# State space phases for half the groups per half of the partitions, on VectorE, and table work dosed behind the weight splits

## The chip, the cores and the metric

One NeuronCore of a Trainium2 chip runs the whole program. The metric is device time in microseconds (us), the median of several runs. TensorE multiplies matrices, VectorE and ScalarE do elementwise work, GpSimd does elementwise work and issues some transfers, SyncE (SP) issues the weight loads.

## What is computed

A stack of three blocks on 256 tokens of 1024 features, in float32: a gated delta rule mixer with a dense SwiGLU feed-forward, a state space (S5) mixer with a mixture of eight experts, and a block of pooling and windowed attention with a wide feed-forward. The change is about the tables of the state space mixer:

```python
dt = exp(log_dt)[:, None]                     # 64 groups, 64 states each
a_bar = exp(lam * dt)                         # complex
b_bar = ((a_bar - 1) / lam)[..., None] * b
h_t = a_bar * h_(t-1) + b_bar u_t             # u: 64 groups of 16 channels
y_t = Re(c h_t) + d * u_t
```

The kernel splits the 256 steps into 64 chunks of four and carries the state from chunk to chunk in a frame that turns with it. For that it needs the phases: the cosine and sine of 4 m Im(lam dt) for m = 0 to 63, for every group and state.

## The kernel before, in words

Weights come from memory in float32 and are used in two parts, a high one (float32r) and the rest. `schedule` lists chunks of 1 MB, two pieces of 128 x 1024 each. `load` (line 296) issues a chunk on SP's queue as soon as one of three buffers is free; `prep` (279) has ScalarE make a piece's high part (290) and VectorE, or GpSimd for the pieces that `pool_splits` names, the low part (292). There are five buffers for parts, and `wget` (314) runs three pieces ahead of the products. `mm3` makes three products of each block (lines 336 to 338).

Side work is written as generators. `spawn` queues one, `tick` (242) runs once for each block of products, and a generator yields how many ticks to let pass. A scheduler at compile time then orders each engine's instructions by the order of the program and by when it expects their inputs; `issue_after` adds an edge that puts an instruction behind another of the same engine. A tile takes the room of an earlier one with the same tag, and waits until nobody uses that one any more.

The dense feed-forward (`ffn`, 967) has 22 blocks of hidden units in groups of 6, 6, 6 and 4. `up(g)` makes a group's hidden units, two pieces and two ticks a block (the first four pieces, two blocks, go tile by tile in `both`, eight ticks, and end in `first`, line 981). `whole(g)` multiplies a group by the second weights, one piece and two ticks a block. The order is up(0), up(1), whole(0), up(2), whole(1), up(3), the loads of the next layer norm's gain and offset (`ln_rows`, 811), whole(2), and the last group, `final`, one token tile after the other. `ln_part` (line 848) adds the residual, `ln_sums` and `ln_apply` (868, 870) normalise, `to_features` (830) turns the rows, and the state space layer `s5` (1235) begins. `ln_rows` loads two rows to one partition on GpSimd's queue (815) and broadcasts them on GpSimd (817). Its tile `gb` shares a tag with `bxy`, and the rows `rr` have the tag `lnr`.

`s5_tables` (1097) runs beside the feed-forward. Four loads are issued at once; six ticks later VectorE begins: two exponentials (`expf`, 1036), a sine and cosine of 448 columns (`sincos`, 1055), powers of the transition, the factor (a - 1) / lam, the input vectors `bxy`, and last the input maps B (1229 to 1232), of which a tick gets one or two operations. The work comes in bunches, with `yield 2` between them. From line 1196 on GpSimd copies six phases (m = 1, 2, 4, 8, 16, 32) into CC and SS and doubles them by products (1209 to 1215), in four generators of 16 groups. Here the partitions hold 64 states twice, once for the real and once for the imaginary part; CC and SS are 128 x 64 groups x 64 chunks, the same in both halves but for a sign in SS.

The pieces that GpSimd splits are 0, 1, 2, 4, 6, 8, 10, 12 of the feed-forward (line 960) and 0, 1, 2 of the state space layer (1032).

Of the kernel before, what the change touches and what calls it, by code (L numbers as in the profile page):

```python
# [42 lines left out]
S5L = dict(per=4, s0=3, m=1, o=0, mb=2, a=2, b=2, c=2, d=4, e=2, f=1, g=1, ct=4, gt=4, keep=2)  # L43
MO = dict(d=3, t=2, b=5, a=2, sc=1)
WARM = dict(a=12, b=9, c=20, e=5, f=0)
MAGIC = 12582912.0
# [32 lines left out]
def _consts():  # L79
    """Masks and index tables that the shapes alone fix, in three groups."""  # L80
# [33 lines left out]
def pack(i):  # L114
    """Device arrays from the inputs: transposes, slices and static gathers only."""
# [13 lines left out]
    # small vectors, features on partitions  # L129
# [10 lines left out]
    # FFN: w1 and w3 block by block  # L140
# [6 lines left out]
    # S5  # L147
# [14 lines left out]
    # experts  # L162
# [9 lines left out]
    # second block  # L172
# [31 lines left out]
class Kern:  # L204
# [16 lines left out]
    # -- small helpers --  # L221
# [15 lines left out]
    def spawn(self, gen, lag=0):  # L237
        """Work that runs beside the weights; it yields how many pieces of weights to let pass."""
# [57 lines left out]
    def load(self, c, upto=None):  # L296
        """Loads as far as the buffers reach while chunk c is in use."""
# [16 lines left out]
    def wget(self):  # L314
        """The next piece of weights (hi, lo); loads and splits run ahead of it."""
# [4 lines left out]
    def hold(self):  # L320
        """Keep the pieces from here on until they are let go."""
# [6 lines left out]
    def split(self, x1, x2, src):  # L328
        """x1 + x2 = src, both float32r."""
# [10 lines left out]
    def colblock(self, out):  # L340
        """out[f, tok] = sum over features of the next 128-column block of weights."""
# [6 lines left out]
    def rsqrt(self, pool, y, v, n):  # L348
        """y = v ** -0.5 for small tiles [128, n], Newton from an integer start."""
# [9 lines left out]
    def rsqrt1(self, y, v, mul, eps):  # L359
        """y = (mul v + eps) ** -0.5 for a few columns: a start from the table, then one Newton step."""  # L360
# [13 lines left out]
    # ------------------------------------------------------------ first layer  # L374
# [29 lines left out]
    def router(self, P):  # L404
        """The router's weights for rows that wait for their layer norm: gain in, mean out; the offset's share with the bias."""
# [22 lines left out]
    def gdn(self):  # L428
# [4 lines left out]
        # chunks of weights that come while the buffers are full of the first ones, in the room of later matrices  # L433
# [13 lines left out]
        def gates():  # L447
            """beta and the log decays, tokens on partitions."""
# [24 lines left out]
            # log1p(e2) = ln(w) e2 / (w - 1), and e2 where w is 1  # L473
# [20 lines left out]
        def until(what, *hs):  # L494
            """Let weights pass until what comes first in the program has been put there."""
# [3 lines left out]
        # decay between every pair of tokens: segments (s0,t0) (s0,t1) (s1,t1)  # L499
# [17 lines left out]
        def project(out, base):  # L517
            """The next 128 channels: causal taps."""
# [7 lines left out]
        def norms(src, v16, h):  # L526
            """silu, and the squared norm of each token."""
# [29 lines left out]
        def gram(h, src):  # L557
            """k_s . src_t for the three segments."""
# [5 lines left out]
        def keyside(h):  # L564
# [9 lines left out]
            # the 16x16 diagonal blocks  # L574
# [25 lines left out]
        def inverse():  # L600
            """Inverses of the diagonal blocks, one block a partition, row by row; then 16 -> 32 -> 64 -> 128."""
# [22 lines left out]
        def levels(*qs):  # L624
# [15 lines left out]
            for m in (16, 32):  # L640
                # both halves of the tokens of a block at once, on different rows of the array
# [55 lines left out]
        def solve(j):  # L697
            """Solve, read out, normalise and gate two heads."""
# [49 lines left out]
        # keys  # L748
# [10 lines left out]
        # gates of the output  # L759
# [6 lines left out]
        # queries  # L766
# [6 lines left out]
        # values  # L773
# [6 lines left out]
        # output projection  # L780
# [40 lines left out]
    def to_features(self, src, t, f32_out=None):  # L821
        """Token-major [128, D] of tile t -> feature-major float32r pair (and float32)."""
# [15 lines left out]
    # ------------------------------------------------------------ residual and layer norm, by parts  # L838
# [1198 lines left out]
```

## Time and profile before

| | us |
|---|---|
| three runs | 1307.24, 1309.83, 1312.06 |
| median | 1309.83 |
| profiled execution, first to last instruction (span) | 1305.7 |
| mean granted TensorE clock in it | 0.981 of full speed |

For the profiled execution only its span is given; its own time with what lies around it is not. A row of the trace has the start and length of an instruction or of a run of them, the engine, the line, what is written and read, and in brackets how long the engine stood idle before it and what it waited for. TensorE's rows are called PE, VectorE's DVE, ScalarE's ACT, GpSimd's POOL. Lengths of neighbouring rows overlap a little.

### The profile page before, as it was taken

Reading aid. Unit: us, or ns where it says so; the run is one execution under the profiler, and the core shown is the slowest. Engines: PE = TensorE matmul, PEld = TensorE weight load, DVE = VectorE, ACT = ScalarE, POOL = GpSimd, SP = SyncE. Lnnn points to the kernel's source line nnn. Section 1 sums busy time; section 2 is a strip of 40 time slices with the busy share of each in tenths; the row PEclk is TensorE's granted clock in tenths of the full one; section 3 lists DMA queues with packets and bytes.
Section 4 is the critical chain, followed back from the end, with each engine's and each line's share of the span. In section 5 each row is a group of like instructions: output and inputs, shape, how many; then the busy total and the mean of one; then the engine's idle time right before and its main releaser. Section 6 shows DMA issues by size and latency. Waiting matters only on the chain. (4 is left out here: it accounts for less than half of the span.)

```text
span 1305.7 us, 19759 instructions
## 1 busy us (share of the span) xinstructions
PE 1230.1 (94%) x7579; PEld 1065.1 (82%) x7579; DVE 1037.9 (79%) x1487; ACT 732.7 (56%) x1086; POOL 353.4 (27%) x321
## 2 busy tenths in 40 slices
PE   8989997998997989899999999999999789999997
PEld 7989876997996777667888888888877677899886
DVE  6677879999865898779998989999988775766553
ACT  6635444442443544448777777767767455655442
POOL 2362014249996656223000000000003371000000
PEclk9989999899998999999999999999999899999999
DMA  8343214453651501136999889899987543455551
GB/s 324 130 138 120 85 65 151 159 188 134 227 194 65 178 33 65 57 130 217 344 343 338 326 322 373 300 333 373 335 302 293 180 151 130 166 190 187 183 189 54
DMA packets 44437, 263.46 MB, mean 202 GB/s; under 512 B 9136, under 2 KB 9536, under 8 KB 18096
## 3 DMA queue, kind: packets, MB, share of 16 engines
q1 hardware_dynamic: 40320, 257.12, 55.2%
q10 hardware_dynamic: 3472, 4.42, 1.0%
q8 instruction: 62, 1.02, 0.3%
q0 software_dynamic: 544, 0.58, 0.1%
q14 instruction: 39, 0.32, 0.1%
HBM read 260.79 MB, written 1.31 MB: 201 GB/s over the span
## 5 line engine op out<-in xcount | busy, mean ns | idle before, releaser
L292 DVE TENSOR_TENSOR wl<-wr,wh 128x1024 fp32r<-128x1024 f32 (+1 forms) x361 | 441.0, 1240 | 125.9 <-ACT wh L290 123.8
L290 ACT ACTIVATE wh<-wr 128x1024 fp32r<-128x1024 f32 (+2 forms) x390 | 391.1, 1025 | 234.4 <-PE po L338 85.8
L338 PE MATMUL pup<-wh,xg 128*128 128x512 f32 (+1 forms) x384 | 145.2, 378 | 2.7 <-PEq L1668 2.4
L337 PE MATMUL pup<-wl,xg 128*128 128x512 f32 (+1 forms) x384 | 146.3, 381 | 0.3 <-DVE wl L292 0.2
L336 PE MATMUL pup<-wh,xg 128*128 128x512 f32 (+1 forms) x384 | 145.9, 380 | 0.0
L292 DVE TENSOR_TENSOR wl<-wx,wh 128x1024 fp32r<-128x1024 f32 (+1 forms) x110 | 122.4, 1146 | 10.5 <-ACT wh L290 8.8
L290 ACT ACTIVATE wh<-wx 128x1024 fp32r<-128x1024 f32 (+1 forms) x112 | 105.0, 980 | 9.9 <-PE pup L338 5.9
L292 POOL TENSOR_TENSOR wl<-wr,wh 128x1024 fp32r<-128x1024 f32 x29 | 76.6, 2656 | 108.3 <-ACT wh L290 77.4
L338 PE MATMUL p<-x,wl 128*128 128x256 f32 x320 | 92.3, 288 | 5.5 <-DVE wl L292 5.3
L336 PE MATMUL p<-x,wh 128*128 128x256 f32 x320 | 91.7, 287 | 0.0
L337 PE MATMUL p<-x,wh 128*128 128x256 f32 x320 | 91.4, 286 | 0.0
L337 PEld LDWEIGHTS pup<-wl,xg 128*128 128x128 f32 x384 | 72.5, 189 | 14.3 <-DVE wl L292 4.0
L338 PEld LDWEIGHTS pup<-wh,xg 128*128 128x128 f32 x384 | 72.6, 189 | 14.1 <-issue 2.8
L336 PEld LDWEIGHTS pup<-wh,xg 128*128 128x128 f32 x384 | 72.8, 190 | 10.9 <-issue 0.2
L337 PE MATMUL pdn<-wl,eh 128*128 128x512 f32 x176 | 69.9, 397 | 0.0
L336 PE MATMUL pdn<-wh,eh 128*128 128x512 f32 x176 | 69.8, 397 | 0.0
L338 PE MATMUL pdn<-wh,eh 128*128 128x512 f32 x176 | 69.5, 395 | 0.0
L338 PEld LDWEIGHTS p<-x,wl 128*128 128x128 f32 x320 | 62.3, 195 | 7.0 <-DVE wl L292 6.9
L336 PE MATMUL pm<-x,wh 128*128 128x256 f32 x224 | 63.5, 283 | 0.0
L338 PE MATMUL pm<-x,wl 128*128 128x256 f32 x224 | 63.4, 283 | 0.0
L337 PE MATMUL pm<-x,wh 128*128 128x256 f32 x224 | 63.4, 283 | 0.0
L336 PEld LDWEIGHTS p<-x,wh 128*128 128x128 f32 x320 | 62.4, 195 | 0.6 <-ACT s L995 0.4
(565 smaller groups left out, 3123.2 us busy)
## 6 DMA issues: line engine op xcount, KB each, us to landing
wr<-w_e SPq DMA_DIRECT2D x59, 1024.0 KB, 6.7
wx<-w_e SPq DMA_DIRECT2D x37, 1024.0 KB, 6.7
wr<-w_f SPq DMA_DIRECT2D x33, 1024.0 KB, 4.8
wr<-w_e SPq DMA_DIRECT2D x29, 768.0 KB, 5.8
wr<-w_up SPq DMA_DIRECT2D x16, 1024.0 KB, 4.9
wr<-w_dn SPq DMA_DIRECT2D x16, 1024.0 KB, 4.9
wx<-w_e SPq DMA_DIRECT2D x19, 768.0 KB, 6.0
wr<-w_glu SPq DMA_DIRECT2D x8, 1024.0 KB, 4.7
```

The lines of the kernel that those rows point to most:

```text
L290: nc.scalar.activation(hi[:, :w], src, AF.Copy)
L292: self.los[self.n_split] = eng.tensor_tensor(lo[:, :w], src, hi[:, :w], op=ALU.subtract)
L336: mm(out, lhsT=l1, rhs=r1, start=start, stop=False)
L337: mm(out, lhsT=l1, rhs=r2, start=False, stop=False)
L338: self.mm = mm(out, lhsT=l2, rhs=r1, start=False, stop=stop)
```

## The change

The doubling products move from GpSimd to VectorE and are formed once for each group: the lower 64 partitions hold the phases of groups 0 to 31, the upper 64 those of groups 32 to 63, in HC and HS (128 x 32 x 64). ScalarE copies the first phases there. Eight transfers on GpSimd's queue then spread them to both halves of CC and SS. HC takes room with the tag `lnr`. The sign that SS had is made in the state space layer, by a factor of -1 in two of its products. The sign of CX moves from GpSimd to ScalarE.

Every operation of `expf`, `sincos` and what follows is put behind the newest weight split on VectorE (`behind`), and `paced` counts columns, plus 64 for each operation, and lets a tick pass for every 1200 of them in `up` and every 650 in `whole`. The tables begin after nine ticks instead of six, the router's weights after 14 instead of 8. GpSimd splits no pieces of the feed-forward. The gain and offset of the layer norm after the feed-forward come to all partitions by one transfer on ScalarE's queue.

```diff
-S5L = dict(per=4, s0=3, m=1, ...)
+S5L = dict(per=4, s0=3, t0=9, m=1, ...)
+PACE = (1200, 650)
...
+    def paced(self, gen):
+        done = 0
+        for size in gen:
+            done += size
+            while done >= self.pace:
+                done -= self.pace
+                yield 1
+
+    def behind(self, f):
+        def run(out, *a, **k):
+            with self.tc.issue_after(self.los[self.n_split - 1].ins):
+                f(out, *a, **k)
+            return 64 + math.prod(out.shape[1:])
+        return run
...
     def ln_rows(self, i, pool, tag, rr=True):
         self.gb = pool.tile([128, 2, D], F32, tag=tag, name="gb")
-        for k in range(2):
-            self.nc.gpsimd.dma_start(self.gb[0:1, k, :], self.a["lnrow"][2 * i + k:2 * i + k + 1, :])
-        for k in range(2):
-            self.nc.gpsimd.partition_broadcast(self.gb[:, k, :], self.gb[0:1, k, :])
+        if i == 1:
+            self.nc.scalar.dma_start(self.gb, self.a["lnrow"][2 * i:2 * i + 2, :].partition_broadcast(128))
+        else:
...
     def plan_ffn(self):
-        self.pool_splits(0, 1, 2, 4, 6, 8, 10, 12)
...
-        self.spawn(self.router(P), 8)
+        self.spawn(self.router(P), 14)
         def up(g):
+            self.pace = PACE[0]
         def whole(g):
+            self.pace = PACE[1]
...
     def expf(self, tmp, out, x):
-        TT, TS, STT = nc.vector.tensor_tensor, nc.vector.tensor_scalar, nc.vector.scalar_tensor_tensor
+        TT, TS, STT = (self.behind(f) for f in (nc.vector.tensor_tensor, nc.vector.tensor_scalar, nc.vector.scalar_tensor_tensor))
-        TS(r, x, 88.0, -87.0, op0=ALU.min, op1=ALU.max)
+        yield TS(r, x, 88.0, -87.0, op0=ALU.min, op1=ALU.max)
...
-        yield 6
+        yield S5L["t0"]
+        yield from self.paced(self.s5_powers(Pt, sm, rbx, rby, wt, temp))
...
-        G.memset(CC[:, :, 0], 1.0)
-        G.memset(SS[:, :, 0], 0.0)
-        for i, m in enumerate(PHASES):
-            G.tensor_copy(CC[:, :, m], ph[:, 0, i, :])
-            G.tensor_copy(SS[:, :, m], ph[:, 1, i, :])
+        HC = self.act.tile([128, 32, NJ], F32, tag="lnr", name="HC")
+        HS = Pt.tile([128, 32, NJ], F32, tag="HS", name="HS", bufs=1)
+        nc.gpsimd.memset(HC[:, :, 0], 1.0)
+        nc.gpsimd.memset(HS[:, :, 0], 0.0)
+        halves = slice(0, 64), slice(64, 128)
+        for i, m in enumerate(PHASES):
+            for h, p in enumerate(halves):
+                o = 64 * (i + 1) + 32 * h
+                nc.scalar.activation(HC[p, :, m], cs[p, o:o + 32], AF.Copy)
+                nc.scalar.activation(HS[p, :, m], sn[p, o:o + 32], AF.Copy)
+            if i % 2:
+                yield self.pace
+        for q in range(2):
             g = slice(16 * q, 16 * q + 16)
             for m in PHASES[1:]:
-                c, s = CC[:, g, 1:m], SS[:, g, 1:m]
+                c, s = HC[:, g, 1:m], HS[:, g, 1:m]
...
-                G.tensor_tensor(co, c, cm, op=ALU.mult)
+                yield TT(co, c, cm, op=ALU.mult)
...
+        for full, half in ((CC, HC), (SS, HS)):
+            for to in halves:
+                for h, p in enumerate(halves):
+                    nc.gpsimd.dma_start(full[to, 32 * h:32 * h + 32, :], half[p])
+        nc.scalar.activation(CX, CX, AF.Copy, scale=sgn)
         for k in range(KT):
...
-            TT(B[:, k], pw(AR), vec(bx), op=ALU.mult)
-            TT(w, pw(AI), vec(by), op=ALU.mult)
-            yield 1
-            TT(B[:, k], B[:, k], w, op=ALU.add)
-            yield 1
+            yield TT(B[:, k], pw(AR), vec(bx), op=ALU.mult)
+            yield TT(w, pw(AI), vec(by), op=ALU.mult)
+            yield TT(B[:, k], B[:, k], w, op=ALU.add)
...
-            TT(q[hi], X[lo], SS[lo, gs, :], op=ALU.mult)
+            STT(q[hi], X[lo], -1.0, SS[lo, gs, :], op0=ALU.mult, op1=ALU.mult)
```

## Rows read from the trace of the kernel before

**Rows 1.** Part 1 of the page: busy us, share, instructions of each engine.

```profile
PE 1230.1 (94%) x7579; PEld 1065.1 (82%) x7579; DVE 1037.9 (79%) x1487; ACT 732.7 (56%) x1086; POOL 353.4 (27%) x321
```

**Rows 2.** Table of stretches: length, busy us by engine, granted clock, DMA share, GB/s.

```profile
229.50:236.00 6.50, 6.45 (x31) 6.05 (x32) 6.17 (x15) 2.45 (x6) 2.42 (x1) 0.54 0.28 120
236.00:249.00 13.00, 13.00 (x110) 13.00 (x110) 13.00 (x30) 6.68 (x10) 7.23 (x1) 1.00 0.55 178
300.00:322.00 22.00, 16.66 (x127) 15.58 (x126) 22.00 (x21) 4.52 (x6) 21.45 (x20) 1.00 0.35 124
345.00:400.00 55.00, 55.00 (x335) 49.48 (x334) 34.82 (x29) 23.92 (x29) 52.96 (x62) 1.00 0.55 187
410.00:424.00 14.00, 5.63 (x27) 5.63 (x27) 9.91 (x14) 3.37 (x6) 4.81 (x3) 0.63 0.00 0
```

**Rows 3.** Timelines near the start of the feed-forward: TensorE, VectorE, GpSimd, ScalarE.

```profile
229.47 1.09 PE L954 MATMUL ptn<-cg,s 128*128 128x128 f32 x4 [5.76 <-DVE s L981]
...
220.93 5.20 DVE L1134 TENSOR_SCALAR SS<-SS 128x64 f32<-128x64 f32 x5
...
228.91 0.74 DVE L981 TENSOR_TENSOR s<-s,ptf 128x256 f32<-128x256 f32 x2
...
221.28 4.70 POOL L292 TENSOR_TENSOR wl<-wr,wh 128x1024 fp32r<-128x1024 f32 x2
...
220.15 0.66 ACT L980 ACTIVATE s<-ptf 128x256 f32<-128x256 f32 x2
```

**Rows 4.** Waits of TensorE from 300 to 322 us: total, times, longest.

```profile
PE p L338 <- DVE wl L292: 5.3, 4, 2.1
```

**Rows 5.** Timelines at both borders, and TensorE's waits from 424 to 432 us.

```profile
418.37 1.12 PE L830 MATMUL ptr<-cg,x 128*128 128x128 f32 x4 [8.99 <-DVE x L870]
...
413.87 2.21 DVE L868 SCALAR_TENSOR_TENSOR lnr<-lnr,lnmv,gb 128x512 f32<-128x512 f32 x2 [8.05 <-POOL gb L817]
...
404.31 1.25 POOL L1215 TENSOR_TENSOR SS<-SS,phw 128x496 f32<-128x496 f32 x1
...
412.54 2.48 POOL L817 PARTITION_BROADCAST gb<-gb  x2 [5.82 <-issue]
...
PE ptf L337 <- POOL wl L292: 1.4, 2, 1.1
...
202.51 0.63 PE L830 MATMUL ptr<-cg,x 128*128 128x128 f32 x4 [1.99 <-DVE x L870]
...
198.83 3.53 DVE L870 SCALAR_TENSOR_TENSOR x<-lnr,lnrs,gb 128x512 f32<-128x512 f32 x2
```

**Rows 6.** Groups by line and form (busy us, mean ns), and VectorE's timeline at 284 us.

```profile
L1049 DVE TENSOR_TENSOR CC<-CC 128x64 f32<-128x64 f32 x12 | 2.6, 220 | 0.2
L1063 DVE SCALAR_TENSOR_TENSOR CC<-SS,CC 128x448 f32<-128x448 f32 x1 | 0.6, 615 | 0.0
L292 DVE TENSOR_TENSOR wl<-wr,wh 128x1024 fp32r<-128x1024 f32 x58 | 82.8, 1429 | 17.5 <-ACT wh L290 17.4
L1209 POOL TENSOR_TENSOR CC<-CC 128x16 f32<-128x16 f32 (+4 forms) x20 | 22.5, 1131 | 0.0
L330 ACT ACTIVATE h<-s 128x256 fp32r<-128x256 f32 x20 | 8.3, 413 | 29.3 <-DVE s L997 29.3
...
284.48 1.08 DVE L1229 TENSOR_TENSOR B<-AR,bxy 128x512 f32<-128x512 f32 x1
285.49 0.41 DVE L331 TENSOR_TENSOR h<-s,h 128x256 fp32r<-128x256 f32 x1
...
286.80 1.21 DVE L292 TENSOR_TENSOR wl<-wr,wh 128x1024 fp32r<-128x1024 f32 x1
287.93 0.70 DVE L1232 TENSOR_TENSOR B<-B,bw 128x512 f32<-128x512 f32 x1
```

**Rows 7.** Transfers: line's tile, queue, count, KB each, median us from issue to landing.

```profile
wr<-w_f SPq DMA_DIRECT2D x33, 1024.0 KB, 4.8
...
CX<-s_cx ACTq DMA_DIRECT2D x1, 512.0 KB, 5.6
```

More of the change, by code (lines that the diff above doesn't have):

```diff
@@ new lines, in expf @@
+        yield TS(k, r, 1.4426950408889634, MAGIC, op0=ALU.mult, op1=ALU.add)
+        yield TS(k, k, -MAGIC, None, op0=ALU.add)
+        yield STT(r, k, -0.693359375, r, op0=ALU.mult, op1=ALU.add)
+        yield STT(r, k, 2.12194440e-4, r, op0=ALU.mult, op1=ALU.add)
+        yield TS(out, r, 1.0 / 5040, 1.0 / 720, op0=ALU.mult, op1=ALU.add)
+        for c in (1.0 / 120, 1.0 / 24, 1.0 / 6, 0.5, 1.0, 1.0):
+            yield TT(out, out, r, op=ALU.mult)
+            yield TS(out, out, c, None, op0=ALU.add)
@@ L1055, in sincos @@
+        yield TS(ki, k, 127.0, None, op0=ALU.add)
+        yield TS(ki, ki, 23, None, op0=ALU.logical_shift_left)
+        yield TT(out, out, ki.bitcast(F32), op=ALU.mult)
     def sincos(self, tmp, s, c, y):
         nc = self.nc
-        TT, TS, STT = nc.vector.tensor_tensor, nc.vector.tensor_scalar, nc.vector.scalar_tensor_tensor
+        TT, TS, STT = (self.behind(f) for f in (nc.vector.tensor_tensor, nc.vector.tensor_scalar, nc.vector.scalar_tensor_tensor))
         k, r, m, z, p, q = tmp
-        TS(k, y, 0.6366197723675814, MAGIC, op0=ALU.mult, op1=ALU.add)
@@ new lines, in sincos @@
+        yield TS(k, k, -MAGIC, None, op0=ALU.add)
+        yield STT(r, k, -1.5703125, y, op0=ALU.mult, op1=ALU.add)
+        yield STT(r, k, -4.837512969970703125e-4, r, op0=ALU.mult, op1=ALU.add)
+        yield STT(r, k, -7.549789948768648e-8, r, op0=ALU.mult, op1=ALU.add)
+        yield TS(m, k, 0.25, MAGIC, op0=ALU.mult, op1=ALU.add)
+        yield TS(m, m, -MAGIC, None, op0=ALU.add)
+        yield STT(m, m, -4.0, k, op0=ALU.mult, op1=ALU.add)
+        yield TT(z, r, r, op=ALU.mult)
+        yield TS(p, z, -1.9515295891e-4, 8.3321608736e-3, op0=ALU.mult, op1=ALU.add)
@@ new lines, in sincos @@
+        yield TT(p, p, z, op=ALU.mult)
+        yield TS(p, p, -1.6666654611e-1, None, op0=ALU.add)
+        yield TT(p, p, z, op=ALU.mult)
+        yield STT(p, p, 1.0, r, op0=ALU.add, op1=ALU.mult)
+        yield TS(q, z, 2.443315711809948e-5, -1.388731625493765e-3, op0=ALU.mult, op1=ALU.add)
+        yield TT(q, q, z, op=ALU.mult)
+        yield TS(q, q, 4.166664568298827e-2, None, op0=ALU.add)
+        yield TT(q, q, z, op=ALU.mult)
+        yield TS(q, q, -0.5, None, op0=ALU.add)
+        yield TT(q, q, z, op=ALU.mult)
@@ new lines, in sincos @@
+        yield TS(q, q, 1.0, None, op0=ALU.add)
+        yield TT(z, m, m, op=ALU.mult)
+        yield TS(r, z, 1.0, None, op0=ALU.is_equal)
+        yield TT(m, m, r, op=ALU.mult)
+        yield TS(z, z, -0.5, 1.0, op0=ALU.mult, op1=ALU.add)
+        yield STT(z, r, -0.5, z, op0=ALU.mult, op1=ALU.add)
+        yield TT(s, m, q, op=ALU.mult)
+        yield TT(r, z, p, op=ALU.mult)
+        yield TT(s, s, r, op=ALU.add)
+        yield TT(c, m, p, op=ALU.mult)
+        yield TT(r, z, q, op=ALU.mult)
@@ L1123, in s5_tables, with s5_powers @@
             nc.scalar.dma_start(d, a[n].rearrange("p (g c) -> p g c", c=16))
-        yield 6
+        yield S5L["t0"]
+        yield from self.paced(self.s5_powers(Pt, sm, rbx, rby, wt, temp))
+    def s5_powers(self, Pt, sm, rbx, rby, wt, temp):
+        nc = self.nc
+        TT, TS, STT = (self.behind(f) for f in (nc.vector.tensor_tensor, nc.vector.tensor_scalar, nc.vector.scalar_tensor_tensor))
+        AR, AI, nAI, rad, B, CC, SS, CX = self.s5t
         lr, li = sm[:, 0, :], sm[:, 1, :]
@@ new lines, in s5_powers @@
+        yield TT(fr, u, lr, op=ALU.mult)
+        yield TT(gs, AI[:, 1, :], li, op=ALU.mult)
+        yield TT(fr, fr, gs, op=ALU.add)
+        yield TT(fr, fr, d, op=ALU.mult)
+        yield TT(fi, AI[:, 1, :], lr, op=ALU.mult)
+        yield TT(gs, u, li, op=ALU.mult)
+        yield TT(fi, fi, gs, op=ALU.subtract)
+        yield TT(fi, fi, d, op=ALU.mult)
+        yield TS(gs, fr, sgn, -1.0, op0=ALU.mult, op1=ALU.mult)
+        yield TS(fs, fi, sgn, -1.0, op0=ALU.mult, op1=ALU.mult)
+        yield TS(nfi, fi, -1.0, None, op0=ALU.mult)
@@ L1214, in phases @@
[L1214 to L1223 removed]
+                yield TT(so, s, cm, op=ALU.mult)
+                yield TT(w, c, sm, op=ALU.mult)
+                yield TT(so, so, w, op=ALU.add)
+        for full, half in ((CC, HC), (SS, HS)):
+            for to in halves:
+                for h, p in enumerate(halves):
+                    nc.gpsimd.dma_start(full[to, 32 * h:32 * h + 32, :], half[p])
```

148 lines of the change are left out of this document (38 added, 110 removed).

## The prediction

> **What bounds the kernel now.** I read the page's shares first, then a table of stretches, then the waits inside the stretches that stood out. The shares [rows 1] show TensorE busy for 94% of the span, so time can only come from where it stops or runs at its lower level. The change touches the dense feed-forward (about 203 to 409 us) and its two borders, and there TensorE loses time in three places.
>
> First, near the start. TensorE stands 5.76 us until VectorE delivers the gated hidden units of line 981 [rows 3], and then runs at half clock: 31 instructions in 6.5 us at a granted 0.54, near 1.2 GHz, against 110 in 13 us at 1.00, 2.4 GHz, just after [rows 2]. VectorE was not idle meanwhile. It ran table operations ahead of line 981, and slowly: five scalings of 64 columns took 5.20 us while GpSimd ran two weight splits in 4.70 us [rows 3]. An operation of 64 columns costs 0.22 us elsewhere [rows 6].
>
> Second, from 300 to 320 us four waits for low parts of weights, 5.3 us together [rows 4]. VectorE is busy for all of 300 to 322 us, and GpSimd, with phases, for 21.45 of the 22 [rows 2].
>
> Third, at the end. GpSimd finishes the phases at 405.56 us. Only then do the two loads and two broadcasts of the layer norm's gain and offset run, behind the phases in its queue, up to 415.02. VectorE's line 868 waits 8.05 us for them, and TensorE 8.99 us for the transposes after it; then come two waits of 1.4 us in all for splits that GpSimd also does late [rows 5]. TensorE restarts at the lower level: the mean grant is 0.63 over 410 to 424 us [rows 2].
>
> **Part by part.** *Start of the feed-forward.* The tables begin nine ticks after their loads instead of six, and each of their VectorE operations is queued behind the newest weight split, in doses. Line 981 is then free of the crowd and the 5.76 us go. At the full rate 31 instructions need 3.7 us, so 2.8 us go with the clock. Gain 8.6 us. What is late next is ScalarE's silu, done at 220.8 us [rows 3], more than two microseconds before TensorE ran out of work.
>
> *The middle.* The 5.3 us of waits go if VectorE is no longer overdrawn. GpSimd, now idle, no longer stretches it (a split takes 1429 ns on average over the feed-forward and 1210 undisturbed [rows 6]), and a dose bounds what a tick gets. Gain 5.3 us, subject to the next item.
>
> *Added to VectorE.* The phases leave GpSimd (six groups of 20 operations, 116.5 us; one of them stands in [rows 6]) and are formed for 32 instead of 64 groups: 60 operations of 16 to 496 columns. From 64 columns in 0.220 and 448 in 0.615 us [rows 6], a column costs 1.03 ns and an operation 0.154 us; 912 columns in 5 operations, six-fold and twice, give 20.5 us. Eight splits also come back, at 1.21 us some 10 us. Against that stands a tick of 24 products, 2.84 us at 110 in 13 us: one split 1.21, one product and one split of hidden units per two ticks 0.41, and a dose of 1200 units, a unit being a column, with 64 more for each operation. In operations of 448 columns a dose takes 1.44 us, in sum 3.06; rows overlap a little (the split begun at 286.80 ends 0.08 us after its follower began), so about 2.8. In those of 64 it takes 2.06, in sum 3.7. The input maps, 1728 units in two operations of 1.08 and one of 0.70 us, give 1.99, in sum 3.6. So the doses fit most ticks, and overdraw by 0.4 to 0.8 us in about 5 ticks at the start and 8 to 15 at the end. Splits are issued three pieces ahead, 8.5 us, which covers a lag of 3 to 7. I take 1 us, with 0 and 6 as its ends.
>
> *End of the feed-forward.* The gain and offset come by one transfer issued from ScalarE, with no broadcast. It lies in the room of bxy, so it waits for the last input map, by ticks some 11 us before line 868. On ScalarE the weight casts queue behind that wait, and VectorE and TensorE wait for the casts, with the same three pieces in hand. The nearest load, 1024 KB, lands in 4.8 us [rows 7]: in time, or a few microseconds late. Gone are 8.99 and 1.4 us, and by the clock some 2.3 (5.6 busy us at about 0.6, an estimate from [rows 2]). What is late next is the chain of the norm itself: at the border before, with its broadcast in time, TensorE waits 1.99 us there [rows 5]. Gain 8.99 + 1.4 + 2.3 - 2.0 = 10.7 us.
>
> *Border before the feed-forward.* VectorE gets two more splits among its norm work, 2.4 us, but the two operations of line 870 that took 3.53 us beside GpSimd's splits [rows 5] fall to some 1.4, by the 0.70 us of a row of their size [rows 6]. I take 0, with -2 and +2.
>
> *Hidden.* Twenty-four copies of 64 by 32 and one scaling on ScalarE, at most 0.41 us each by [rows 6], spread over three ticks and more: ScalarE is busy for 23.9 of 55 us there [rows 2]; without that slack the splits would wait. Products with a factor of -1 instead of without: the three-operand form takes 0.615 us where a plain one of its size is 0.61 too, so nothing. Eight transfers of 512 KB on GpSimd's queue: nothing needs them until the layer norm takes HC's room at line 848, some 42 us after the phases end (8 ticks of 2.84, six pieces of 2.7, a first half of 2.7), and then the state scan. The nearest row, 512 KB, lands in 5.6 us with two others in flight [rows 7]: four of HC in 22 us, all eight in 45. Behind them in that queue stand only the state space layer's splits; SP's queue is not passed.
>
> In this trace GpSimd and VectorE slow each other, 1.04 us for what takes 0.22 [rows 3, 6]. The Trainium skill, page "SBUF — State Buffer", section "A bandwidth-pool intuition that's wrong (but worth ruling out)", has a rule that speaks against the change: a transfer issued from GpSimd has its descriptors written by that engine, and a VectorE operation in a two-port mode locks it out, so that some 620 ns become 3100. No transfer in this trace is issued from GpSimd under a busy VectorE, so nothing here shows it. By that page eight issues would take 20 us more, an estimate from its figures, and still be in time; the sum would not change.
>
> **Sum.** 8.6 + 5.3 + 10.7 + 0 - 1 = 23.6 us off the profiled span of 1305.7 us: 1282.1. The median of the runs, 1309.83, lies 4.1 us above that span and the lowest run 1.5. I take the gain off the median: 1286.
>
> **Rivals.** *VectorE becomes the bound, or gain and offset come late* (0.17): the overdraft exceeds the lead of three pieces, or bxy is freed so late that line 868 still waits. For it: VectorE is filled from 236 to 249 and from 300 to 322 us already. Against: it is busy for only 34.8 of 55 us from 345 to 400 [rows 2], where most of the new work goes. Price: the upper end of 6 us for the overdraft, 5 for a late load and its clock, and both with -2 at the first border: gains of 11 to 17, so 1293 to 1299, 1302 with the first row's 2.8 us of clock lost too.
>
> *The tables were not the cause at the start* (0.06), or something unseen gives the gain back (0.06): line 981 still waits behind splits, and the unfinished maps hold the border as the broadcasts did. Two of the three gains fall, less than 6.5 us stays: about 1305. Against: rows 3 name no other work in VectorE's way.
>
> *Slower: the spread* (0.07). Line 848's first write needs HC's room; VectorE stands there, and all that is behind it. It decides if HC's four transfers take over 42 us, 10.5 each, twice the 5.6 of the row. To end above 1316 the gain of 23.6 and 6.5 more must go: 72 us for four, 18 each. For it: half the partitions, and some 170 GB/s of weights beside it [rows 2]. Against: that is three times the nearest row. Price, at 20 us each: 80 - 42 = 38 us, 1286 + 38 = 1324. The page's lock would add its 2.5 us to each issue here.
>
> **How the numbers follow.** The forecast has 0.64. About 0.5%, 6.5 us, is what a measurement of this kernel can tell from no change. Forecast and first rival end faster by more than that: 0.81. Same 0.12, slower 0.07. Gains at their best (8.6 + 5.3 + 12.7 + 2.0, nothing given up at the norm's chain) give 1281, and relief of VectorE that I have not counted 1277; costs at their worst end the first rival at 1302. Range 1277 to 1302.
>
> **What would show it.** Right: no wait at line 954 near 229 us, none for low parts between 280 and 330, line 868 not waiting for gain and offset, a grant of 1.00 across both borders, GpSimd nearly idle in the feed-forward. The doses are wrong if TensorE waits for line 292 near the feed-forward's end; the new load if line 868 waits for a DMA; the spread if line 848 does. If all shows right and the time still stays above 1300, the gain was given back in the state space layer, and I am wrong about what follows the border.

## The result, and the profile after

| | us |
|---|---|
| kernel before, median of 4 runs | 1309.30 |
| changed kernel, median of 4 runs (1290.76 to 1296.16) | 1294.95 |
| ratio | 0.9881, 95% interval 0.9862 to 0.9900 |
| profiled execution of the changed kernel: time, span | 1290.76, 1289.0 |

The change is faster by 1.2%, 14.4 us between the medians. The forecast was 1286, so some 9 us are missing. The profiled execution is the shortest of the four. The same kernel was profiled once more, beside the later experiments: span 1293.9, median 1295.41. What lies between its two profiles is told at the end.

Shares of the span (the page of the changed kernel; answers to [rows 1]):

```profile
PE 1229.2 (95%) x7579; PEld 1064.0 (83%) x7579; DVE 1028.2 (80%) x1553; ACT 739.0 (57%) x1111; POOL 199.5 (15%) x184
```

GpSimd lost 154 us of work (353.4 before). VectorE runs 66 instructions more, yet is busy for 9.7 us less (1037.9 before). The same stretches as in [rows 2], from the windows table of the changed kernel (busy us and instructions of each engine, granted clock, share of the transfer engines, GB/s):

```profile
229.50:236.00 6.50, 6.50 (x57) 6.50 (x56) 5.93 (x25) 2.91 (x5) 0.00 (x0) 1.00 0.46 165
300.00:322.00 22.00, 22.00 (x186) 22.00 (x185) 20.07 (x46) 10.30 (x16) 0.00 (x0) 1.00 0.53 192
345.00:400.00 55.00, 51.30 (x304) 43.60 (x303) 46.86 (x58) 21.24 (x27) 5.81 (x3) 1.00 0.86 240
410.00:424.00 14.00, 12.84 (x56) 10.85 (x57) 6.34 (x10) 6.12 (x10) 6.48 (x7) 0.88 0.11 39
```

In the first two, TensorE now works all the time at 1.00, 2.4 GHz: the half clock after line 954's wait is gone. In the third it is busy for 51.30 of 55 us, the rest being the border, which comes earlier now, and late products ahead of it. In the fourth the clock is better (0.63 before) but not full; and the border itself has moved: over 396 to 404, 404 to 412 and 412 to 425 us the grant is 0.80, 0.71 and 0.91.

Where the time went is read from landmarks of the two timelines, the starts of certain products:

| stretch | before | after | gain | predicted |
|---|---|---|---|---|
| to the last first-column product (border before) | 217.3 | 217.4 | -0.1 | 0 |
| from there to the first product with second weights | 67.4 | 58.9 | 8.5 | 8.6 (start) |
| from there to the last column product | 97.2 | 90.2 | 7.0 | 5.3 (middle) |
| from the product behind it to the last product of the feed-forward (the tail) | 27.0 | 30.6 | -3.6 | -1 (overdraft) |
| from there to the first following column of the state space layer (the border) | 32.4 | 28.0 | 4.4 | 10.7 (end) |
| the rest | | | 0.4 | |

The first half came as forecast, the middle 1.7 us better. The tail cost 2.6 us more than expected and the border gave 6.3 us less, 8.9 in all. In this pair of profiles, whose spans differ by 16.7 us, that leaves the sum of 23.6 short by 6.9, since the middle and the rest give some 2 back; the 9 us by which the median misses is nearly the same number, but not the same account.

**The tail.** Transfer issues from 330 to 420 us in the changed kernel (KB each, median us from issue to landing; [rows 7] answer):

```profile
wr<-w_f SPq DMA_DIRECT2D x7, 1024.0 KB, 11.4
CC<-HC POOLq DMA_DIRECT2D x4, 512.0 KB, 11.9
SS<-HS POOLq DMA_DIRECT2D x4, 512.0 KB, 27.1
gb<-lnrow ACTq DMA_DIRECT2D x1, 1024.0 KB, 6.3
```

and waits between 340 and 397 us (us in total, times, longest):

```profile
ACT wh L308 <- DMA wr<-w_f: 18.1, 3, 8.0
ACT wh L308 <- DVE bw L264: 3.4, 1, 3.4
```

Weights land in 11.4 us instead of 4.8, ScalarE's casts wait 18.1 us for them, and six of the tail's 120 products start 0.2 to 1.0 us late, with those right behind them by 3.4 us in all: 2.0 up to 383 us, behind late weights, and 1.4 from 385 to 389. The second row is the block that gain and offset put on ScalarE's queue; it ends at 383.7, and the later part follows it. TensorE's waits from 362 to 397 us:

```profile
PE po L355 <- DVE wl L310: 1.5, 5, 0.8
```

**The border.** The timeline of the changed kernel across it (start, length, engine, line, operation; idle time before it and what ended it):

```profile
393.84 1.41 DVE L890 SCALAR_TENSOR_TENSOR lnr<-lnr,lnmv,gb 128x512 f32<-128x512 f32 x2
...
396.67 5.12 POOL L310 TENSOR_TENSOR wl<-wr,wh 128x1024 fp32r<-128x1024 f32 x2 [5.92 <-DVE lnrs L390]
396.67 5.67 DVE L892 SCALAR_TENSOR_TENSOR x<-lnr,lnrs,gb 128x512 f32<-128x512 f32 x2
397.09 0.39 PE L356 MATMUL po<-wh,h 128*128 128x512 f32 x1
399.64 0.66 PE L852 MATMUL ptr<-cg,x 128*128 128x128 f32 x4 [2.17 <-DVE x L892]
...
402.40 1.12 PE L852 MATMUL ptr<-cg,x 128*128 128x128 f32 x4 [1.88 <-DVE x L892]
...
411.16 1.97 PE L852 MATMUL ptr<-cg,x 128*128 128x128 f32 x8 [2.78 <-DVE x L892]
...
411.93 1.08 ACT L1278 ACTIVATE BT<-pbt 128x512 f32<-128x512 f32 x2 [4.48 <-DVE x L892]
412.78 0.78 PE L354 MATMUL ptf<-wh,x 128*128 128x512 f32 x1
...
425.06 0.28 PE L354 MATMUL pu<-x,wh 128*128 128x256 f32 x1
```

Line 890 (868 before) waits for nothing any more: gain and offset are there. But the two operations of line 892 take 5.67 us where such a pair took 1.41 at line 890, and they start with two splits on GpSimd. And TensorE's order has turned: the transposes of token tile 1 (411.16) stand ahead of tile 0's 24 products (412.78); before, those products ran first, at 425.23, and the transposes at 434.06. The row of ScalarE's copy BT, late behind line 892, looks like a bystander here; it is not.

### The profile page after: what moved, and what is told of

Read it like the earlier page. It is cut to its first block, busy times and chain, and to the rows that moved or that the text cites. A ratio compares the mean times of both kernels' runs of the same rounds, so it can differ in the third digit from the quotient of the medians.

```text
span 1289.0 us, 19749 instructions
## 1 busy us (share of the span) xinstructions
PE 1229.2 (95%) x7579; PEld 1064.0 (83%) x7579; DVE 1028.2 (80%) x1553; ACT 739.0 (57%) x1111; POOL 199.5 (15%) x184
## 3 DMA queue, kind: packets, MB, share of 16 engines
q1 hardware_dynamic: 40320, 257.12, 54.7%
## 5 line engine op out<-in xcount | busy, mean ns | idle before, releaser
L310 DVE TENSOR_TENSOR wl<-wr,wh 128x1024 fp32r<-128x1024 f32 (+1 forms) x369 | 434.7, 1195 | 126.9 <-ACT wh L308 124.1
L310 POOL TENSOR_TENSOR wl<-wr,wh 128x1024 fp32r<-128x1024 f32 x21 | 50.7, 2434 | 109.9 <-ACT wh L308 104.0
L354 PEld LDWEIGHTS p<-x,wh 128*128 128x128 f32 x320 | 61.4, 192 | 0.6 <-ACT s L1017 0.5
L355 PEld LDWEIGHTS p<-x,wh 128*128 128x128 f32 x320 | 61.4, 192 | 0.1
```

The lines of the kernel that those rows point to most:

```text
L310: self.los[self.n_split] = eng.tensor_tensor(lo[:, :w], src, hi[:, :w], op=ALU.subtract)
L354: mm(out, lhsT=l1, rhs=r1, start=start, stop=False)
L355: mm(out, lhsT=l1, rhs=r2, start=False, stop=False)
```

## The experiments

All timed runs in one table. Tail and border are as above, in us of the profiled execution; "columns" is from the feed-forward's last product to the last of the layer's input columns, since some orders mix products of tile 1 with the first of them.

| run | median | ratio to before [95%] | profiled span | tail | border | columns |
|---|---|---|---|---|---|---|
| before | 1309.30 | 1 | 1305.7 | 27.0 | 32.4 | 57.9 |
| changed | 1294.95 | 0.9881 [0.9862, 0.9900] | 1289.0 | 30.6 | 28.0 | 54.3 |
| changed again | 1295.41 | 0.9887 [0.9862, 0.9911] | 1293.9 | 30.2 | 28.3 | 54.6 |
| VectorE makes the splits | 1288.12 | 0.9845 [0.9814, 0.9876] | 1286.6 | 30.3 | 25.2 | 51.5 |
| tile 0 first | 1295.70 | 0.9898 [0.9872, 0.9924] | 1293.4 | 30.1 | 25.8 | 57.2 |
| both | 1293.84 | 0.9880 [0.9864, 0.9897] | 1292.0 | 30.1 | 22.7 | 54.1 |
| half of the spread | 1288.19 | 0.9862 [0.9822, 0.9902] | 1286.0 | 27.4 | 28.0 | 54.7 |
| room | 1290.63 | 0.9849 [0.9825, 0.9874] | 1289.3 | 30.7 | 23.9 | 50.2 |
| room, splits | 1282.95 | 0.9793 [0.9769, 0.9817] | 1285.2 | 30.3 | 19.0 | 44.8 |
| room, splits, half of the spread | 1281.40 | 0.9783 [0.9759, 0.9806] | 1279.9 | 27.4 | 19.0 | 44.7 |
| no doses | 1350.75 | 1.0327 [1.0307, 1.0347] | 1349.3 | 27.0 | 27.8 | 54.1 |
| GpSimd splits at the start | 1291.50 | 0.9866 [0.9850, 0.9882] | 1289.6 | 29.9 | 27.6 | 53.9 |
| before, gain and offset alone | 1302.17 | 0.9953 [0.9936, 0.9969] | 1298.6 | 27.0 | 24.6 | 50.5 |
| phases on GpSimd | 1298.82 | 0.9927 [0.9908, 0.9946] | 1297.8 | 29.7 | 28.0 | 54.4 |

### The border: splits, order, room

Two theories at first. A: GpSimd's splits stretch VectorE's line 892. B: TensorE's order costs the gain.

```diff
     def plan_s5(self):
-        self.pool_splits(0, 1, 2)
```

> The changed kernel, but VectorE makes the first three weight splits of the state space layer that GpSimd made. Theory A (the two splits on GpSimd that start with VectorE's last step of the norm stretch that step from 1.4 to 5.7 us, and TensorE waits for it): the pair takes 1.4 us again, one split of 1.2 us now stands before it, and the chain to the second tile's transposes (411.2 us) is 2 to 3 us shorter; time 1291 to 1293. Theory B (the order on TensorE alone costs the gain: transposes of tile 1 stand ahead of tile 0's products): the pair may get shorter, but the first product of the layer moves by less than 1 us; time 1294 to 1296.

The pair of line 892 takes 1.41 us again and the border is 2.8 us shorter. From the timeline of this run:

```profile
398.71 1.41 DVE L892 SCALAR_TENSOR_TENSOR x<-lnr,lnrs,gb 128x512 f32<-128x512 f32 x2
...
409.26 1.97 PE L852 MATMUL ptr<-cg,x 128*128 128x128 f32 x8 [5.35 <-DVE x L892]
```

A holds, by its own size. The median is 6.8 us below that of the changed kernel, which was not run beside it, and below the 1291 to 1293 expected; the border has only 2.8 of it. Against the second profile of the changed kernel (span 1293.9) this one is 7.2 us shorter: 3.1 at the border and 4.2 behind it, most of that in the layer's second half, where that profile falls to the lower clock and this one does not (told at the end). A wait of 5.35 us is left ahead of the transposes of tile 1.

```diff
-        self.to_features(self.src(1), 1)
-        for t in range(2):
-            self.spawn(first(t, self.tokfirst(t)))
+        pb0 = self.tokfirst(0)
+        with self.tc.issue_after(self.mm.ins):
+            self.to_features(self.src(1), 1)
+        self.spawn(first(0, pb0))
+        self.spawn(first(1, self.tokfirst(1)))
```

> The changed kernel, but the eight transposes of token tile 1 at the start of the state space layer are ordered behind the 24 products of tile 0. Theory A (GpSimd's splits are what costs): the wait of 2.78 us ahead of the transposes goes, but tile 0's features are late because of the stretched step, so tile 0's products start no more than 3 us earlier (412.8 to about 410); the stretched pair stays at 5.7 us; time 1292 to 1294. Theory B (the order is what costs): tile 0's products start at about 408.5, right behind the input maps, the wait of 2.78 us is gone and the first product of the columns that follow comes 4 us earlier (425.1 to 421); time 1290 to 1291.

> The two edits together: VectorE makes the three splits, and tile 0's products stand ahead of tile 1's transposes. If both mechanisms count and add, tile 0's products start at about 405 us and the following columns 6 us earlier than in the changed kernel (425.1 to 419): the border falls from 28.0 to 22 us, the 21.6 that the prediction's 10.7 us asked for; time 1288 to 1290. If only one counts, no better than the better one alone.

Neither gives the time that B, or A and B together, asked for. In the second the border shrinks to 22.7 us, but the columns end where they ended before (54.1 us, 54.3 in the changed kernel). Tile 0's products stand first now, and wait all the same. Their first row, alone and with the splits on VectorE:

```profile
411.87 0.80 PE L354 MATMUL ptf<-wh,x 128*128 128x512 f32 x1 [4.19 <-ACT BT L1278]
```

```profile
409.08 0.80 PE L354 MATMUL ptf<-wh,x 128*128 128x512 f32 x1 [6.69 <-ACT BT L1277]
```

What they wait for is ScalarE's copy BT, the transposed input map: it frees the PSUM bank that these products write. So the order was not the cause, B falls, and forcing it left TensorE idle where the transposes had filled in. But why is BT late? In the changed kernel it waits 4.48 us for VectorE's line 892 (above), whose data it does not use. The built programs list the semaphores that the first BT waits for:

```
before    PE
changed   DMASW3 DMASW4 DMASW2 DMASW5 DVE DMAHW2 PE Pool
room      DMASW3 DMASW4 DMASW2 DMASW5 PE Pool
```

(The last line belongs to the run with the room, below.) DMASW are queues of transfers issued from GpSimd, here the four that spread HS; DMAHW2 is that of gain and offset (line 890 waits for it too), Pool the first write of HS on GpSimd. DVE is VectorE, up to the last operation of line 892, for tile 1: the last reader of gain and offset. The addresses of the tiles say where they come from: the new tile HS lies at 188384 to 196576 bytes of each partition, right behind gain and offset (180192 to 188384), and moves the hidden units up by 8192. BT is at 193440 before and after. There hidden units of the first and third group lay before, and now lies HS. This is theory C.

```diff
-        HS = Pt.tile([128, 32, NJ], F32, tag="HS", name="HS", bufs=1)
+        HS = P2.tile([128, 32, NJ], F32, tag="HS", name="HS", bufs=1)
```

(P2 is the pool of the hidden units; HS comes to lie behind them, and BT's room is under hidden units again.)

> The changed kernel with one tile moved: the sine phases' half table HS lies in the room that it leaves free above the hidden units, no longer where the state space layer's transposed input maps (BT) come. Theory C (new: because BT lies where HS lay, ScalarE's first BT waits at 411.2 us for the norm's last step of tile 1, it keeps its PSUM bank until then, and the 24 products of tile 0 need that bank; so neither order nor splits alone can bring them): BT is copied at about 404 to 407 us, tile 0's products start right behind the input maps at 408.5 (412.8 before), the transposes of tile 1 fall behind them by themselves, and the first following column comes at 420 to 422 instead of 425.1; VectorE's pair beside GpSimd's splits stays at 5.7 us; time 3 to 5 us below the changed kernel. Theory A (GpSimd's splits alone): no more than 1 us.

> HS moved, and VectorE makes the three weight splits. Theory C with A: TensorE waits neither for the stretched pair nor for the bank; tile 0's products start at 404 to 405, the first following column at 417 to 419; the border is 20 to 22 us instead of 28, what the prediction's 10.7 us asked for; time 6 to 8 us below the changed kernel. Theory A alone: 1 us below the run with the splits alone, 2 to 3 below the changed kernel in the profiled span.

With HS moved the list is shorter by DVE and DMAHW2, BT is copied 6.2 us earlier, and the compile-time scheduler puts tile 0's products first by itself. From the timeline of the run with the room alone:

```profile
405.72 0.59 ACT L1278 ACTIVATE BT<-pbt 128x512 f32<-128x512 f32 x1
...
407.17 1.95 PE L1284 MATMUL pk<-CX,B 128*128 128x128 f32 x8
408.87 0.48 PE L354 MATMUL ptf<-wh,x 128*128 128x512 f32 x1
```

They start behind the input maps' last product (pk), without a wait. The border falls from 28.3 to 23.9, and with VectorE's splits to 19.0, below the 21.6 that the prediction asked for. Medians of the same chip: 1295.41, 1290.63, 1282.95. The last is 12.5 us below the first where 6 to 8 were expected; 9.3 of it are the border. C is shown, and A beside it. The turned order was a consequence of the late bank. Why must a copy into HS's old room also wait for the last reader of gain and offset, which lie beside it? The list of the run with the room points to the pool. It still names HS's four transfers and its first write, though HS there lies at 219104 to 227296, clear of BT (193440 to 195488), in the same pool as the hidden units under BT. In the changed kernel BT comes into the room of the pool that holds both HS and gain and offset, and waits for the users of both. So the wait seems to go by the pool whose room a tile enters, not by the bytes under it; two lists say so, and no run tried a third place.

### The tail: the spread beside the weights

```diff
                 for h, p in enumerate(halves):
-                    nc.gpsimd.dma_start(full[to, 32 * h:32 * h + 32, :], half[p])
+                    if p == to:
+                        nc.scalar.activation(full[to, 32 * h:32 * h + 32, :], half[p], AF.Copy)
+                    else:
+                        nc.gpsimd.dma_start(full[to, 32 * h:32 * h + 32, :], half[p])
```

> The changed kernel, but of the eight transfers that spread the phases the four that stay on their own partitions are copies on ScalarE. Theory A (the spread fills the transfer engines, the weights behind it land in 11.4 us instead of 4.8, and ScalarE's casts and TensorE wait for them late in the feed-forward): the landing of weights falls to 6 to 8 us, the three waits of ScalarE's casts for weights, 18.1 us, fall below half, and the last product of the feed-forward comes 1 to 3 us earlier (397.1 to 394 to 396); time 1292 to 1294. Theory B (VectorE's input maps that run until 384 us hold the splits): the landing falls likewise but the last product stays at 397 or is later, since ScalarE has 8 us of copies more.

Theory A of this pair holds; the time, 1288.19, is below its 1292 to 1294, of which the tail explains some 3 us. Transfer issues from 330 to 420 us, then a wait between 340 and 397 us:

```profile
wr<-w_f SPq DMA_DIRECT2D x7, 1024.0 KB, 6.0
SS<-HS POOLq DMA_DIRECT2D x2, 512.0 KB, 12.7
```

```profile
ACT wh L308 <- DMA wr<-w_f: 5.6, 2, 4.6
```

The tail is 27.4 us, 0.4 above that of before, and TensorE's waits for low parts there are gone, although the doses and the input maps on VectorE are the same. The scheduler also moved some of VectorE's operations in this kernel, so the share of that is not separated; the four copies of 1.9 us on ScalarE cost nothing that shows.

### The changed kernel again, and all three edits

> The changed kernel as it is, beside the three that follow, on one chip: every theory expects its own time again, 1291 to 1296, with the border from the feed-forward's last product to the first following column at 28 us.

> HS moved, VectorE makes the splits, and half of the spread is copied by ScalarE. If the three mechanisms are separate, the gains add: the last product of the feed-forward 3 us earlier than in the run without the lighter spread, the border as there, time 9 to 11 us below the changed kernel, 1281 to 1285: the 23.6 us of the prediction's sum would be had in full. If the copies on ScalarE disturb the norm, no better than the run before.

The gains add: tail 27.4, border 19.0, and 14.0 us between the medians of one chip, more than the 9 to 11 expected. The spans of the two profiles differ by the same 14.0; tail and border make 12.1 of it, and the rest lies mainly behind the border. Between the medians of this run and the one without the lighter spread there are only 1.6 us, where the tail gives 2.9. TensorE's only wait within the border, and two of the border's stretches:

```profile
407.73 1.32 PE L852 MATMUL ptr<-cg,x 128*128 128x128 f32 x8 [0.34 <-DVE x L892]
```

```profile
396.00:404.00 8.00, 8.00 (x44) 7.48 (x43) 8.00 (x11) 4.74 (x8) 3.33 (x2) 1.00 0.46 144
404.00:412.00 8.00, 7.65 (x38) 5.83 (x38) 6.32 (x12) 4.03 (x6) 0.85 (x3) 1.00 0.50 185
```

The grant is 1.00 across the border, as the prediction wanted to see it. This version is some 2% below the kernel before (1281.40 against 1308.06 beside it).

### The terms of the prediction, one at a time

```diff
-PACE = (1200, 650)
+PACE = (10 ** 9, 10 ** 9)
```

> The changed kernel without the doses: all table operations from the first to the last come in one tick (three where the copies pause), each still behind the newest weight split. If the doses carry the gain of start and middle: low parts of weights and gated units come late between 222 and 330 us, TensorE waits 5 to 14 us there, and the feed-forward's last column product comes at 371 to 380 us instead of 366 to 368; time 1299 to 1309. If the order behind a split and an idle GpSimd are enough: 366 to 369 us, and no more than 2 us above the changed kernel.

Far more than expected, 42 us above the kernel before (1308.5 beside it). One wait on TensorE makes most of it:

```profile
303.43 0.58 PE L354 MATMUL p<-x,wh 128*128 128x256 f32 x1 [42.66 <-DVE s L1019]
```

All table operations hang on one early split, stand together on VectorE, and the gated unit of line 1019 comes when they are through. So the doses are what keeps the tables from stopping TensorE; order behind a split is not enough. But the gain of the start does not hang on them. Up to 250 us this kernel, too, has no wait for line 954's operand (976 here), and the first stretch of [rows 2] runs at full clock:

```profile
229.50:236.00 6.50, 6.50 (x56) 6.50 (x56) 4.91 (x14) 3.75 (x7) 0.00 (x0) 1.00 0.40 129
```

Line 981's operation (1002 here) runs at 222.65 us and the tables' first at 223.32; in the kernel before the tables began at 213.57, fifteen us ahead of line 981. What lifts the first wait is that the tables come behind it, by the later begin or the order behind a split; these two were not separated.

```diff
     def plan_ffn(self):
+        self.pool_splits(0, 1, 2, 4, 6, 8, 10, 12)
```

> The changed kernel with the eight weight splits at the start of the feed-forward on GpSimd again (0, 1, 2, 4, 6, 8, 10, 12), as in the kernel before. If GpSimd beside VectorE is what made the start slow: the pair of the norm's last step takes 3.5 us instead of 1.4, small table operations 1 us instead of 0.2 while a split runs, TensorE waits 2 to 6 us between 217 and 232 us and falls to half clock, and the last column product comes at 370 to 375 us. If the delay and the order of the table operations made it: no more than 1.5 us later than in the changed kernel, 366 to 369.

The pair at the border before is stretched as expected (VectorE's timeline):

```profile
198.47 3.53 DVE L892 SCALAR_TENSOR_TENSOR x<-lnr,lnrs,gb 128x512 f32<-128x512 f32 x2
...
230.91 2.42 DVE L264 TENSOR_SCALAR CC<-CC 128x64 f32<-128x64 f32 x1
233.26 0.69 DVE L264 TENSOR_SCALAR SS<-SS 128x64 f32<-128x64 f32 x6
```

and so is one small table operation (2.42 us beside a split of 2.40), but the last column product is at 366.1 us, as in the changed kernel, and TensorE waits 0.25 us at 224. So, with the tables late and in doses, taking splits off GpSimd there neither gained nor cost anything that shows. In the kernel before it may have counted: the five scalings of [rows 3] took 5.20 us where six take 0.69 here, and line 981 stood behind them. The kernel before without GpSimd's splits was not run.

```diff
+        if i == 1:
+            self.nc.scalar.dma_start(self.gb, self.a["lnrow"][2 * i:2 * i + 2, :].partition_broadcast(128))
+        else:
             for k in range(2):
                 self.nc.gpsimd.dma_start(self.gb[0:1, k, :], self.a["lnrow"][2 * i + k:2 * i + k + 1, :])
...
```

> The kernel before with one part of the change alone: the gain and offset of the second layer norm come by one transfer from ScalarE's queue, with no broadcast on GpSimd; the phases stay on GpSimd until 405 us. The prediction's own term: the wait of 8.05 us at the norm's first step and TensorE's 8.99 us go, and the border from last product to first following column falls from 32.3 us to 21.6 to 24; time 1299 to 1302. Theory A (splits that GpSimd still makes right then stretch the norm's steps on VectorE and come late themselves): only to 26 to 29; time 1302 to 1306.

In between: the border is 24.6 us. The norm's steps stand beside GpSimd's splits (timeline):

```profile
405.93 2.40 POOL L292 TENSOR_TENSOR wl<-wr,wh 128x1024 fp32r<-128x1024 f32 x1
...
406.99 2.55 DVE L871 SCALAR_TENSOR_TENSOR lnr<-lnr,lnmv,gb 128x512 f32<-128x512 f32 x2
...
409.82 4.67 POOL L292 TENSOR_TENSOR wl<-wr,wh 128x1024 fp32r<-128x1024 f32 x2 [1.50 <-ACT wh L290]
...
410.05 2.16 DVE L368 SCALAR_TENSOR_TENSOR rs<-lnrs,rs 128x1 f32<-128x1 f32 x1
...
412.74 1.77 DVE L372 SCALAR_TENSOR_TENSOR lnrs<-rs,lnrs 128x1 f32<-128x1 f32 x1
...
415.35 1.12 PE L833 MATMUL ptr<-cg,x 128*128 128x128 f32 x4 [4.73 <-DVE x L873]
```

8.99 us became 4.73, not 2.0. The two operations of one column, 0.21 and 0.15 us at the border before (208.43 and 209.23 us in the kernel before), take 2.16 and 1.77. In this kernel, without HS, this edit by itself gives 7.8 us at the border, where the whole change gives 4.4.

```diff
-                yield TT(co, c, cm, op=ALU.mult)
+                GT(co, c, cm, op=ALU.mult)
...
+                yield 6 * (64 + 16 * (m - 1))
```

(All six products and sums of a doubling step, GT being GpSimd's.)

> The changed kernel, but the halved phases (60 operations) are formed on GpSimd instead of VectorE: 58 us by half of the 116.5 us of before, or less where VectorE is calm. If moving them to VectorE matters: they end near 370 us, the spread is issued some 30 us later, its transfers land near 395 to 400 us, and the first write of the norm's rows (389 us), which need HC's room, waits 5 to 12 us for it; two-input operations on VectorE are stretched while GpSimd works (1.2 us splits to 1.4 on average); time 1300 to 1310. If halving them and the rest of the change do it: the norm waits for nothing, 1293 to 1297.

The time is just below the first case's, and by another way: the phases end at 335.3 us, not 370, so the spread is issued 5 us earlier than in the changed kernel (333.3 for 338.3) and the norm waits for nothing. What is lost lies in the middle. TensorE waits for low parts again, and VectorE's splits from 295 to 335 us take 1647 ns on average where the changed kernel's take 1220:

```profile
301.50 0.38 PE L356 MATMUL p<-x,wl 128*128 128x256 f32 x1 [2.81 <-DVE wl L310]
```

```profile
L310 DVE TENSOR_TENSOR wl<-wr,wh 128x1024 fp32r<-128x1024 f32 x16 | 26.3, 1647 | 0.0
```

The last column product comes at 376.0, 8.4 to 9.6 us later than in the changed kernel. Moving the phases is worth the middle of the sum, and a little more.

## Why the prediction was right, and where its sum was off

Start, 8.6 us: right in size, 8.5 measured, and in both its parts: TensorE's idle time in this stretch falls from 5.9 to 0.3 us and its busy time, at the higher clock, from 61.5 to 58.6. Of the mechanism the prediction named three pieces, later begin, order and doses; the run without doses shows that the first two are enough. Silu was late next, as said: TensorE waits 0.26 us at 224. Whether lifting GpSimd's splits alone would have done it, too, is open.

Middle, 5.3 us: 7.0 measured, and the run with the phases on GpSimd shows that a GpSimd that is idle there makes it.

Added to VectorE, -1 with ends 0 and -6: 54 of the phases' operations average 0.31 us and the last six take 0.67, 21 us in all, for 20.5 in the sum. With half of the spread the tail loses 0.4 us, so the overdraft was sized well. The prediction's own sign said otherwise: the doses are wrong if TensorE waits for line 292 near the end, and it does, five times, 1.5 us in all. With the same doses and half of the spread these waits are gone, so the sign did not tell the doses from the transfers. The 3.6 us of the tail belong to another step, the eight transfers. The prediction costed them at nothing because nobody waits for them soon, and that was right: HC's four landed 20 us after the first was issued, of 42 allowed, so the slower rival's condition was far off. What it missed is who shares the transfer engines with them. Its row [rows 7], 4.8 us for a load of weights, was used for gain and offset and never asked of the weights themselves. The first step of the sum that failed is therefore "hidden: eight transfers": held at nothing, they took some 3 us of the tail. (The block on ScalarE's queue, which the prediction weighed, stands in the run with half of the spread too, ending at 381.9 us, and the tail's products are late there by 0.3 us in all. So it cost something only behind late weights.)

End of the feed-forward, 10.7 us: the second step that failed. Gain and offset were in time (landed 6.3 us after 383.26, used at 393.84), as the term said. "Late next is the chain of the norm itself, 1.99 us there" was wrong twice. It took the row of a border where GpSimd's splits stretch the same pair, 3.53 us in [rows 5], and here it left such splits on GpSimd; they now meet the first tile's last step exactly, 5.67 us. And it did not look at where a new 8 KB tile would lie, and who would come into its room. Without these two the term is 32.4 - 19.0 = 13.4 us, more than its 10.7. The grant of 1.00 across this border, which it named as a sign, came only then.

Border before, 0: right, 0.1; the run with GpSimd's splits there agrees.

The first rival's number, 1293 to 1299, holds the measured time, but neither of its reasons was at work: VectorE was not overdrawn beyond its lead and gain and offset were not late. The range, 1277 to 1302, holds because it is wide, not because the sum was right: tail and border failed by 9 us together, and that the middle and the rest gave 2 back was luck. With the two misses mended, the median lies 26.7 us below that of before on the same chip (1308.06 to 1281.40), of which the sum of 23.6 would explain nearly all.

The Trainium skill, page "SBUF — State Buffer", section "Who interferes with whom", says that a VectorE instruction with two inputs from SBUF and a GpSimd instruction that reads SBUF exclude each other for a whole instruction. This trace agrees: a first operation of line 892 takes 2.91 us where the split beside it takes 2.37, and 0.7 alone. The lock on descriptor writing that the prediction weighed is not seen: between 338.3 and 344.3 us, where the eight transfers are issued, VectorE is busy for 6.00 of 6 us, and the issues take 4.28 us of GpSimd, 0.54 each. Whether any of VectorE's operations there, all with two inputs, ran in the two-port mode that the rule asks for, no trace shows; so the rule is not tested.

## What to carry to other kernels

A new tile in a stacked pool has two prices, its bytes and the next stage's tiles that come to lie in the room of its pool: compare addresses and the wait lists of the next stage's first writers before and after. A term that names several causes at once is right in size without telling which of them worked; take them away one at a time. A transfer that nobody waits for still slows those that somebody does, so ask for the landing time of the weights beside it. When an order on an engine turns, look first for what made the old order impossible; forcing it back only moves the wait.

## What was unexpected of the hardware

Transfers from 64 partitions to 64 fill the transfer engines and move little more than weights alone. Windows of the changed kernel, before and during the spread:

```profile
310.00:338.00 28.00, 28.00 (x193) 26.14 (x192) 27.62 (x69) 12.74 (x17) 0.00 (x0) 1.00 0.52 189
345.00:353.00 8.00, 8.00 (x69) 8.00 (x68) 8.00 (x10) 3.55 (x5) 0.00 (x0) 1.00 1.04 220
```

A share of 0.52 moved 189 GB/s with weights alone, and twice the share only 220 with the spread. The Trainium skill, page "SBUF — State Buffer", section "Door 1: The DMA port swizzle", states that 64 partitions reach only half of the ports; the rows agree, though no run here separates the ports from another cause.

The exclusion works in both directions and for tiny operations. GpSimd's timeline with the phases there, one form twice, the first beside a product of 1024 columns on VectorE:

```profile
299.15 1.08 POOL L1232 TENSOR_TENSOR phw<-HS 128x16 f32<-128x16 f32 x1
301.62 0.27 POOL L1236 TENSOR_TENSOR phw<-HC,HS 128x16 f32<-128x16 f32 x1
```

And the same wait need not have the same price. In the changed kernel TensorE stands 2.9 us near 525 us in both profiles. The row that ends the wait and the stretch behind it, in the first profile and in the second:

```profile
525.01 1.12 PE L1354 MATMUL pyi<-B,CC 128*64 128x64 f32 x16 [2.90 <-DVE CC L1342]
...
526.00:530.00 4.00, 4.00 (x26) 3.43 (x24) 1.42 (x2) 0.71 (x2) 0.00 (x0) 1.00 0.00 0
```

```profile
526.09 1.94 PE L1354 MATMUL pyi<-B,CC 128*64 128x64 f32 x16 [2.91 <-DVE CC L1342]
...
526.00:530.00 4.00, 3.91 (x21) 3.45 (x22) 1.56 (x2) 1.80 (x4) 0.00 (x0) 0.50 0.00 0
```

One execution stays at 2.4 GHz, the other falls to 1.2, and the layer's second half takes 101.9 us instead of 99.1. That is 2.8 of the 4.9 us between the two spans, so the profiled pair of the result is kinder to the change than the second profile would be; the medians decide. The profiles of the other runs are of both kinds (the run with VectorE's splits stays at 1.00 there), so two of them, or two medians, can differ by more than tail and border show.
